# Attention's loads on GpSimd's DMA queue, and its result in a buffer of its own, in a hybrid diffusion layer

## Chip, cores and metric

One core of one Trainium2 chip runs the whole program. The metric is device microseconds (us) from start to end of one execution; lower is better.

## The reference, cut to what matters

One layer acts on 256 context tokens and 2048 latent tokens (a grid of 32 rows by 64 columns), both 1024 wide. After a modulated RMSNorm one projection of 8192 columns feeds three mixers (attention, a gated linear recurrence, a short convolution) and the gates that merge them; two more projections and a last RMSNorm follow. Everything is float32. The part that matters here is attention with its gate:

```python
(q, k, v, g_na, u, g_lru, c_b, c_c, c_h, g_conv,
 m_na, m_lru, m_conv) = jnp.split(xm @ w_in, SPLIT_IDX, axis=-1)
...
s_loc = einsum('brnqhd,brnikhd->brnhqik', q_blk, k_band)   # 8 x 16 window in an 8 x 32 band
s_ctx = einsum('brnqhd,bchd->brnhqc', q_blk, ctx_k)        # 256 cached context keys
p = softmax(concat([s_loc * scale + bias, s_ctx * scale]))
o_na = p_loc @ v_band + p_ctx @ ctx_v
...
merged = sigmoid(m_na) * ((o_na * silu(g_na)) @ w_br_na) + ...
```

There are 8 heads of 64. Context tokens attend densely to the 256 context tokens.

## The kernel before, in words

**Dense work.** The input projection is done by `dense` (L197): `load_w` (L138) loads a tile of 128 output columns in two halves (`wraw`, L143, on SyncE's queue, SP), ScalarE casts each half to its high part `whi` (L55) and GpSimd subtracts to get the low part `wlo` (L56). `w_in_chunk` (L147) then makes 24 matmuls of 128x512 (L153; three per slice of 128 inputs, the third of which needs `wlo`) and a function of the tile moves the result out of PSUM. In the stages below that is `ev_tanh` (L164): ScalarE writes `evm` (L167) and issues its store to `d_sig` on its own DMA queue (L168).

**Side work.** Attention is a generator of units that `dense` steps through `Side.tick` (L187) between chunks. In stage A (about 650 to 1015 us of the trace: 20 tiles of 3 chunks, one unit after each chunk) it does the context tokens (`prompt_steps`, L657: 8 heads, 2 units each) and the first group of 512 latent tokens. In stage B (about 1588 to 2047 us: tiles of 2 chunks, 101/27 units after each chunk) it does the other three groups of latent tokens. Stage B begins with a call of `first_loads` (L862), two tiles with no side work, and then 14 tiles with it.

**A job** is one group of one head (L737; 8 jobs in A, 24 in B) and has four units of 128 queries. `attend1` (L575) makes the scores: two matmuls against the cached keys (`sc`, L583), two against the band (`sl`, L587), then maximum, exponential and scaling on VectorE and ScalarE (L588 to L598). `attend2` (L601) transposes the probabilities (L611) and copies them (L614), `attend3` (L618) multiplies by the values (L624). A unit's later steps lag its first by two to four units (`unit`, L628, and `advance`, L635). After a job's last unit `fin` (L757) multiplies the sums by the gate: two VectorE instructions (L761) write over `sg`, and SP stores `sg` to `d_z` (L762).

**The loads.** `load_head` (L711) loads a head's keys `kd` (L715) and cached keys `ck` (L717), `load_values` (L720) its values `vb` (L722), `load_group` (L725) a job's queries `qs` (L728), its bias `bt` where that is new (L731) and its gate `sg` (L734). They are called after unit 0 of the job before (L784 to L787; the values after unit 3, L788). `first_loads` (L739) loads what the first job needs, with `cv` (L742). In `prompt_steps`, `load` (L661) loads queries, keys and gate of a head (L665 to L667), and L672 the context values. All are issued by SP, in one queue with `wraw` and the stores. Queries come through `twice` (L654), which reads the same 64 rows of `d_q` twice, into partitions 0 to 63 and 64 to 127: its outermost dimension is a 2 that steps nowhere. `qs`, `kd`, `ck`, `vb`, `bt` have two buffers each, `sg` has five. So queries of job j+1 take the buffer of job j-1, which is free once the last `sl` matmul of job j-1 has read it.

What sets the order is each engine's own queue: an instruction that waits for a buffer or a semaphore holds up all behind it on that engine. The order in a queue follows the program's, with small shifts made when it is built.

Of the kernel before, what the change touches and what calls it, by code (L numbers as in the profile page):

```python
# [7 lines left out]
F32 = mybir.dt.float32  # L8
# [3 lines left out]
ALU = mybir.AluOpType  # L12
# [3 lines left out]
P = 128  # L16
# [11 lines left out]
HD = 64  # L28
# [16 lines left out]
def build(nc, tc, H):  # L45
    es = ExitStack()
    V, S, G, TE, SY = nc.vector, nc.scalar, nc.gpsimd, nc.tensor, nc.sync
# [3 lines left out]
    def r2f(ap):  # L51
        return ap.bitcast(F32)
# [20 lines left out]
    def scratch(name, shape):  # L73
        return tc.dram_tile(shape, F32, name=name)
# [3 lines left out]
    d_q, d_k = scratch("d_q", [512, 2, T]), scratch("d_k", [HEADS, 2, HD, T])  # L78
    d_ck = scratch("d_ck", [HEADS, 2, HD, 256])
    d_v = scratch("d_v", [NCTX, 512])  # L80


    d_vb = scratch("d_vb", [HEADS, P, 8, 4, HD])
    d_gna = scratch("d_gna", [512, T])
# [3 lines left out]
    d_z = scratch("d_z", [1536, T])  # L88
# [30 lines left out]
    def bank(name):  # L119
        return psA.tile([P, 512], F32, tag="bank", name=name, bufs=8)  # L120
# [115 lines left out]
    with tc.tile_pool(name="p0", bufs=2) as p0:  # L236
# [23 lines left out]
        for i in range(4):  # L260
            mr_ = p0.tile([P, 512], F32, tag="tm", name=f"mrow{i}", bufs=3)
            (V.tensor_copy if i % 2 else S.copy)(mr_[:2, :], pm[i][:2, :])
            for j in range(4):
                o = 2 * (4 * i + j)
# [363 lines left out]
    def unit(nm, qs, keys, bias, pv, oap, nloc, fin=None):  # L628

        p = attend1(nm, qs, keys, bias, nloc)  # L630
        pend.append((nm, p, pv, oap, fin))
        if len(pend) > DEPTH:
            advance()
# [17 lines left out]
    def rows(h):  # L651
        return slice(h * HD, h * HD + HD)

    def twice(h, t0, n):  # L654
        return d_q[rows(h), :, t0 : t0 + n].unsqueeze(0).broadcast_to([2, HD, 2, n])

    def prompt_steps(pp, first_loads):  # L657

        ts = {}

        def load(h):  # L661
            qp = pp.tile([P, 2, 256], F32R, tag="qp", name=f"qp{h}")
            kp = pp.tile([P, 256], F32R, tag="ck", name=f"kp{h}")
            sp = pp.tile([HD, 256], F32, tag="sp", name=f"sp{h}", bufs=3)
            SY.dma_start(r2f(qp), twice(h, 0, 256))  # L665
            SY.dma_start(r2f(kp), d_k[h, :, :, 0:256].rearrange("a p n -> (a p) n"))
            SY.dma_start(sp, d_gna[rows(h), 0:256])  # L667
            ts[h] = qp, kp, sp

        load(0)  # L670
        vpr = pp.tile([P, 2, 512], F32, tag="vpr", name="vpr", bufs=1)
        SY.dma_start(vpr, d_v[0:256, :].rearrange("(a p) c -> p a c", p=P))  # L672
        for _ in range(8):
            yield
        for h in range(HEADS):
            if h == 1:
                first_loads()
            if h + 1 < HEADS:
                load(h + 1)
            qp, kp, sp = ts.pop(h)  # L680
            o = bank(f"op{h}")

            def fin(sp=sp, o=o, h=h):
                for a in range(2):
                    V.scalar_tensor_tensor(sp[:, a * P : (a + 1) * P], o[a * HD : a * HD + HD, a * P : (a + 1) * P],
                                           0.5, sp[:, a * P : (a + 1) * P], ALU.mult, ALU.mult)
                SY.dma_start(d_z[rows(h), 0:256], sp)

            for a in range(2):
                def oap(q0, q1, a=a, o=o):  # L690
                    return o[a * HD : a * HD + HD, a * P + q0 : a * P + q1]
                unit(f"p{h}_{a}", [qp[:, i, a * P : (a + 1) * P] for i in (0, 1)], [kp], None,
                     [[(c * P, vpr[:, c, rows(h)], P, 0, P) for c in range(2)]], oap, 0,
                     fin if a == 1 else None)
                yield
# [6 lines left out]
    def latent_steps(at, gs):  # L702

        cv = at.tile([P, 2, 512], F32, tag="cv", name=f"cv{gs[0]}", bufs=1)
        row0 = GR[gs[0]][1]
        nrows = GR[gs[-1]][1] + GR[gs[-1]][2] - row0
        nrow_max = max(GR[g][2] for g in gs)
        nq = (nrows + 3) // 4
        heads, groups, bias = {}, {}, {}

        def load_head(h):  # L711

            kd = at.tile([P, nrows * 64], F32R, tag="kd", name=f"kd{row0}_{h}")
            t0 = 256 + row0 * 64
            SY.dma_start(r2f(kd), d_k[h, :, :, t0 : t0 + nrows * 64].rearrange("a p n -> (a p) n"))  # L715
            ck = at.tile([P, 256], F32R, tag="ck", name=f"ck{row0}_{h}")
            SY.dma_start(r2f(ck), d_ck[h].rearrange("a p n -> (a p) n"))  # L717
            heads[h] = [kd, ck, None]

        def load_values(h):  # L720
            vb = at.tile([P, nq, 4, HD], F32, tag="vb", name=f"vb{row0}_{h}")
            SY.dma_start(vb, d_vb[h][:, row0 // 4 : row0 // 4 + nq])  # L722
            heads[h][2] = vb

        def load_group(g, h):  # L725
            _, _, nrow, bi = GR[g]
            qs = at.tile([P, 2, 512], F32R, tag="qs", name=f"qs{g}_{h}")
            SY.dma_start(r2f(qs), twice(h, 256 + 512 * g, 512))  # L728
            if (bi, h) not in bias:
                bt = at.tile([P, 3, nrow_max * 32], F32, tag="bt", name=f"bt{bi}_{h}")  # L730
                SY.dma_start(bt[:, :, : nrow * 32], H[f"bias{bi}"][h])  # L731
                bias[bi, h] = bt
            sg = at.tile([HD, 512], F32, tag="sg", name=f"sg{g}_{h}", bufs=5)
            SY.dma_start(sg, d_gna[rows(h), 256 + 512 * g : 768 + 512 * g])  # L734
            groups[g, h] = qs, bias[bi, h], sg

        jobs = [(g, h) for h in range(HEADS) for g in gs]  # L737

        def first_loads():  # L739
            load_head(0)  # L740
            load_group(*jobs[0])
            SY.dma_start(cv, H["cv"].rearrange("(a p) c -> p a c", p=P))  # L742
            load_values(0)

        return first_loads, latent_units(at, jobs, heads, groups, cv, row0, load_head, load_group, load_values)

    def latent_units(at, jobs, heads, groups, cv, row0, load_head, load_group, load_values):
        for ji, (g, h) in enumerate(jobs):
            (kd, ck, vb), (qs, bt, sg) = heads[h], groups.pop((g, h))
            _, kr0, nrow, _ = GR[g]  # L750
            nloc = nrow * 32
            o = bank(f"o{h}_{g}")
            ov = o.rearrange("p (r c) -> p r c", c=64)
            kv = kd[:, (kr0 - row0) * 64 : (kr0 - row0 + nrow) * 64].rearrange("p (r c) -> p r c", c=64)
            q0_ = (kr0 - row0) // 4

            def fin(o=o, sg=sg, g=g, h=h):  # L757
                for a in (0, 1):
                    ga, oa = (x.rearrange("p (r b c) -> p r b c", b=4, c=16)[:, :, a::2, :]
                              for x in (sg, o[a * HD : a * HD + HD]))  # L760
                    V.scalar_tensor_tensor(ga, oa, 0.5, ga, ALU.mult, ALU.mult)  # L761
                SY.dma_start(d_z[rows(h), 256 + g * 512 : 256 + (g + 1) * 512], sg)  # L762

            nxt = jobs[ji + 1] if ji + 1 < len(jobs) else None
            for b in range(4):
                def oap(q0, q1, b=b, ov=ov):
                    h0 = b % 2 * HD
                    return ov[h0 : h0 + HD, q0 // 16 : q1 // 16, 16 * b : 16 * b + 16]
                pv = []
                for c, q0, q1 in FULL.get(g, MID):  # L770
                    keys = min(4, nrow - 4 * c) * 32
                    pv.append((c * P, vb[:, q0_ + c, b, :], keys, q0, q1))
                for c in range(2):
                    pv.append((nloc + c * P, cv[:, c, rows(h)], P, 0, P))

                fu = [x for x in pv if x[4] - x[3] == P]
                hv = [x for x in pv if x[4] - x[3] < P]
                pv = [fu[:3] + hv[:1], fu[3:] + hv[1:]] if len(hv) == 2 else [fu, hv]
                ct = (0, 1, 1, 2)[b]
                unit(f"{h}_{g}_{b}", [qs[:, i, b * P : (b + 1) * P] for i in (0, 1)],  # L780
                     [kv[:, :, BS[b] : BS[b] + 32], ck], bt[:, ct, :nloc], pv, oap, nloc,
                     fin if b == 3 else None)

                if nxt and b == 0:  # L784
                    if nxt[1] != h:
                        load_head(nxt[1])
                    load_group(*nxt)  # L787
                if nxt and b == 3:  # L788
                    if nxt[1] != h:
                        load_values(nxt[1])  # L790
                yield
# [118 lines left out]
    with tc.tile_pool(name="zp", bufs=2, reuse_waits="tile") as zp:  # L910
        for c in (0, 1, 2, 3, 4):
            t0, n = CH[c]
# [4 lines left out]
            for br in (2, 1, 0):  # L917
# [6 lines left out]
                for m in range(8):  # L924
                    t = zp.tile([P, 512], F32, tag="acc" if br == 2 else "tg", name=f"tg{c}_{br}_{m}",
                                bufs=9 if br == 2 else 6)
# [20 lines left out]
    with tc.tile_pool(name="op", bufs=2, reuse_waits="tile") as op:  # L947
# [17 lines left out]
        for t1, n1 in [(0, P), (P, P)] + [(256 * c, 256) for c in range(1, T // 256)]:  # L965
            if t1:
                mh, ml = nxt if t1 == P else load_m(t1, n1)
            for j in range(n1 // P):
                t0 = t1 + j * P
# [105 lines left out]
```

## Time and profile before

| what | value |
|---|---|
| median of 3 runs | 2635.49 us (2634.15 to 2640.91) |
| the profiled execution's own time | 2634.21 us |
| its span in the trace | 2632.4 us |
| PE (TensorE matmul) busy | 2542.0 us, 97% of the span |
| DVE (VectorE), ACT (ScalarE), POOL (GpSimd) busy | 1092.2, 977.5, 720.6 us |
| moved by DMA | 360.55 MB, mean 137 GB/s |

Times are us unless marked ns. PEld is TensorE's weight load. A name such as `qs<-d_q` is output<-input; L728 is a line of the kernel; SPq and ACTq are the instruction queues of SyncE and ScalarE when they issue DMAs. The time of a DMA issue is how long it held its queue, not how long the data took. A busy figure counts no DMA issues. PEclk is the granted TensorE clock as a share of 2.4 GHz; the levels are 2.4 and 1.2 GHz, so 0.93 is a mean over stretches at 1 and at 0.5.

### The profile page before, as it was taken

Reading aid. Unit: us, or ns where it says so; the run is one execution under the profiler, and the core shown is the slowest. Engines: PE = TensorE matmul, PEld = TensorE weight load, DVE = VectorE, ACT = ScalarE, POOL = GpSimd, SP = SyncE. Lnnn points to the kernel's source line nnn. Section 1 sums busy time; section 2 is a strip of 40 time slices with the busy share of each in tenths; the row PEclk is TensorE's granted clock in tenths of the full one; section 3 lists DMA queues with packets and bytes.
Section 4 is the critical chain, followed back from the end, with each engine's and each line's share of the span. In section 5 each row is a group of like instructions: output and inputs, shape, how many; then the busy total and the mean of one; then the engine's idle time right before and its main releaser. Section 6 shows DMA issues by size and latency. Waiting matters only on the chain.

```text
span 2632.4 us, 35267 instructions
## 1 busy us (share of the span) xinstructions
PE 2542.0 (97%) x13192; PEld 2077.3 (79%) x13192; DVE 1092.2 (41%) x2329; ACT 977.5 (37%) x1849; POOL 720.6 (27%) x594
## 2 busy tenths in 40 slices
PE   8999999999699999999999998899889999999998
PEld 4887788888688888888888886677677888888887
DVE  5101344555023332324877862445445134333433
ACT  4312353444133334435665653344444311111221
POOL 2311223332111111521544441000000413334642
PEclk9999999999899999999999998999999999999999
DMA  7335642332533433335643335444442466545442
GB/s 272 111 90 154 180 113 79 74 69 68 156 118 123 138 123 142 125 107 139 185 157 99 114 120 167 131 140 145 142 132 91 142 216 217 176 156 172 165 144 88
DMA packets 228796, 360.55 MB, mean 137 GB/s; under 512 B 55945, under 2 KB 100617, under 8 KB 227601
## 3 DMA queue, kind: packets, MB, share of 16 engines
q1 hardware_dynamic: 175264, 291.17, 36.4%
q10 hardware_dynamic: 53360, 67.13, 7.6%
q8 instruction: 104, 1.70, 0.3%
q14 instruction: 68, 0.55, 0.1%
HBM read 248.10 MB, written 110.11 MB: 136 GB/s over the span
## 4 chain that ended last, share of the span: by engine, by line
PE 77%; DMA 9%; SPq 1%; DVE 1%; ACT 1%; issue 0%; POOL 0%; ACTq 0%; DVEq 0%; POOLq 0%
PE ps L153 45%; PE pb L931 12%; PE po L980 8%; DMA qs<-d_q 5%; PE t L611 3%; PE o L624 3%; PE pg L454 2%; PE pv L321 2%; PE sl L587 1%; PE sc L583 1%; DMA bt<-bias 1%; DMA kd<-d_k 1%; DMA cv<-cv 1%; DMA o_st<-h 0%; SPq L734 0%
## 5 line engine op out<-in xcount | busy, mean ns | idle before, releaser
L153 PE MATMUL ps<-xh,whi 128*128 128x512 f32 (+1 forms) x2400 | 898.1, 374 | 0.0
L153 PE MATMUL ps<-xl,whi 128*128 128x512 f32 (+1 forms) x2400 | 887.5, 370 | 2.1 <-DVE xl L56 1.6
L153 PE MATMUL ps<-xh,wlo 128*128 128x512 f32 (+1 forms) x2400 | 886.9, 370 | 0.0
L56 POOL TENSOR_TENSOR wlo<-wraw,whi 128x512 fp32r<-128x512 f32 x240 | 333.8, 1408 | 1085.6 <-ACT whi L55 998.6
L153 PEld LDWEIGHTS ps<-xh,whi 128*128 128x128 f32 x2400 | 454.5, 189 | 93.1 <-ACT qo L367 5.2
L153 PEld LDWEIGHTS ps<-xl,whi 128*128 128x128 f32 x2400 | 454.8, 189 | 78.3 <-POOL xl L56 2.5
L153 PEld LDWEIGHTS ps<-xh,wlo 128*128 128x128 f32 x2400 | 454.4, 189 | 77.3
L55 ACT CAST whi<-wraw 128x512 fp32r<-128x512 f32 x240 | 144.8, 616 | 320.0 <-PE ps L153 182.7
L931 PE MATMUL pb<-zh,wbh 128*128 128x512 f32 (+1 forms) x480 | 179.4, 374 | 4.3 <-ACT zh L55 4.3
L931 PE MATMUL pb<-zl,wbh 128*128 128x512 f32 (+1 forms) x480 | 179.7, 374 | 0.0
L931 PE MATMUL pb<-zh,wbl 128*128 128x512 f32 (+1 forms) x480 | 179.6, 374 | 0.0
L167 ACT ACTIVATE evm<-ps 128x512 f32<-128x512 f32 (+1 forms) x120 | 66.3, 553 | 301.1 <-PE ps L153 264.9
L588 DVE TENSOR_SCALAR_CACHE_REDUCE p<-sc 128x256 f32<-128x256 f32 x127 | 53.9, 424 | 274.4 <-PE sc L583 273.5
L938 POOL TENSOR_TENSOR tg<-tg,tg 128x512 f32<-128x512 f32 (+1 forms) x80 | 97.6, 1228 | 189.4 <-DVE tg L934 183.9
L934 DVE SCALAR_TENSOR_TENSOR tg<-tg,pb 128x512 f32<-128x512 f32 (+1 forms) x120 | 75.0, 631 | 158.6 <-PE pb L931 146.2
L611 PE MATMUL t<-ident,p 128*128 128x128 f32 (+1 forms) x698 | 129.2, 285 | 3.6 <-DVE ast L595 1.6
L611 PEld LDWEIGHTS t<-ident,p 128*128 128x128 f32 (+1 forms) x698 | 91.4, 142 | 50.9 <-issue 19.7
L614 ACT COPY pT<-t 128x512 f32<-128x512 f32 (+3 forms) x256 | 96.2, 407 | 85.1 <-PE t L611 83.1
L596 ACT ACTIVATE p<-p,ast 128x736 f32<-128x736 f32 (+2 forms) x127 | 109.5, 862 | 41.8 <-DVE ast L595 38.8
L444 DVE SCALAR_TENSOR_TENSOR uf<-ut,pk,uf 128x512 f32<-128x512 f32 (+1 forms) x120 | 104.2, 868 | 31.4 <-ACT uf L441 29.4
L55 ACT CAST zh<-zr 128x512 fp32r<-128x512 f32 (+1 forms) x60 | 30.5, 575 | 213.3 <-PE pb L931 134.7
L931 PEld LDWEIGHTS pb<-zh,wbh 128*128 128x128 f32 x480 | 90.7, 189 | 22.1 <-ACT zh L55 4.8
(222 smaller groups left out, 3494.9 us busy)
## 6 DMA issues: line engine op xcount, KB each, us to landing
wraw<-w_in SPq DMA_DIRECT2D x240, 256.0 KB
d_sig<-evm ACTq DMA_DIRECT2D x96, 256.0 KB
tg<-d_sig SPq DMA_DIRECT2D x96, 256.0 KB
xt<-x SPq DMA_DIRECT2D x36, 512.0 KB
qs<-d_q SPq DMA_DIRECT2D x32, 512.0 KB
zr<-d_z SPq DMA_DIRECT2D x12, 1024.0 KB
d_mrg<-tg ACTq DMA_DIRECT2D x32, 256.0 KB
mr<-d_mrg SPq DMA_DIRECT2D x8, 1024.0 KB
```

What stands on the lines that cost most here:

```text
L55: S.copy(hi, src)
L56: lo_eng.tensor_tensor(lo, src, r2f(hi), ALU.subtract)
L153: TE.matmul(ps[:, :n], (lo if a else hi)[:, k, :], (xl if b else xh)[ci][:, k, :], start=(i == 0), stop=(i == len(ps_) - 1))
L444: V.scalar_tensor_tensor(uf[:, :n], ut[:, tap : tap + n], cw(tap), uf[:, :n], ALU.mult, ALU.add)
L596: S.activation(p[:, :nk], p[:, :nk], AF.Exp, bias=st[:, 2:3], accum_out=st[:, 3:4])
L611: TE.transpose(tb[:, off : off + w], p[q0:q1, c0 : c0 + P], ident[q0:q1, q0:q1])
L614: S.copy(pT[:, base : base + off], tb[:, :off])
L624: TE.matmul(o, lhsT, rhs, start=(i == 0), stop=(i == len(todo) - 1))
L931: TE.matmul(ps[:, :n], (wbl if a_ else wbh)[br * 4 + k][:, m * P : (m + 1) * P], (zl if b_ else zh)[:, k, :n], start=(i == 0), stop=(i == ...
L934: V.scalar_tensor_tensor(t[:, :n], t[:, :n], 1.0, ps[:, :n], ALU.add, ALU.mult)
L938: G.tensor_tensor(acc[m][:, :n], acc[m][:, :n], t[:, :n], ALU.add)
L980: TE.matmul(ps, (ml if a_ else mh)[:, k, j * P : (j + 1) * P], (wol if b_ else woh)[k][:, hs], start=(i == 0), stop=(i == len(ps_) - 1))
```

## The change

Every load of attention is issued by GpSimd's queue in place of SP's: three per head and one more in `prompt_steps`, and in the latent part `kd`, `ck`, `vb`, `qs`, `bt`, `sg` and `cv`. `fin` writes to a new tile `zt` (two buffers) and SP stores that; `sg` has three buffers in place of five. Stores and the loads of weights stay on SP. No arithmetic changes.

```diff
@@ prompt_steps, load
-            SY.dma_start(r2f(qp), twice(h, 0, 256))
-            SY.dma_start(r2f(kp), d_k[h, :, :, 0:256].rearrange("a p n -> (a p) n"))
-            SY.dma_start(sp, d_gna[rows(h), 0:256])
+            G.dma_start(r2f(qp), twice(h, 0, 256))
+            G.dma_start(r2f(kp), d_k[h, :, :, 0:256].rearrange("a p n -> (a p) n"))
+            G.dma_start(sp, d_gna[rows(h), 0:256])
...
-        SY.dma_start(vpr, d_v[0:256, :].rearrange("(a p) c -> p a c", p=P))
+        G.dma_start(vpr, d_v[0:256, :].rearrange("(a p) c -> p a c", p=P))
@@ latent_steps
-            SY.dma_start(r2f(kd), d_k[h, :, :, t0 : t0 + nrows * 64].rearrange("a p n -> (a p) n"))
+            G.dma_start(r2f(kd), d_k[h, :, :, t0 : t0 + nrows * 64].rearrange("a p n -> (a p) n"))
...
-            SY.dma_start(r2f(ck), d_ck[h].rearrange("a p n -> (a p) n"))
+            G.dma_start(r2f(ck), d_ck[h].rearrange("a p n -> (a p) n"))
...
-            SY.dma_start(vb, d_vb[h][:, row0 // 4 : row0 // 4 + nq])
+            G.dma_start(vb, d_vb[h][:, row0 // 4 : row0 // 4 + nq])
...
-            SY.dma_start(r2f(qs), twice(h, 256 + 512 * g, 512))
+            G.dma_start(r2f(qs), twice(h, 256 + 512 * g, 512))
...
-                SY.dma_start(bt[:, :, : nrow * 32], H[f"bias{bi}"][h])
+                G.dma_start(bt[:, :, : nrow * 32], H[f"bias{bi}"][h])
...
-            sg = at.tile([HD, 512], F32, tag="sg", name=f"sg{g}_{h}", bufs=5)
-            SY.dma_start(sg, d_gna[rows(h), 256 + 512 * g : 768 + 512 * g])
+            sg = at.tile([HD, 512], F32, tag="sg", name=f"sg{g}_{h}", bufs=3)
+            G.dma_start(sg, d_gna[rows(h), 256 + 512 * g : 768 + 512 * g])
...
-            SY.dma_start(cv, H["cv"].rearrange("(a p) c -> p a c", p=P))
+            G.dma_start(cv, H["cv"].rearrange("(a p) c -> p a c", p=P))
@@ latent_units, fin
+                zt = at.tile([HD, 512], F32, tag="zt", name=f"zt{g}_{h}")
                 for a in (0, 1):
-                    ga, oa = (x.rearrange("p (r b c) -> p r b c", b=4, c=16)[:, :, a::2, :]
-                              for x in (sg, o[a * HD : a * HD + HD]))
-                    V.scalar_tensor_tensor(ga, oa, 0.5, ga, ALU.mult, ALU.mult)
-                SY.dma_start(d_z[rows(h), 256 + g * 512 : 256 + (g + 1) * 512], sg)
+                    za, ga, oa = (x.rearrange("p (r b c) -> p r b c", b=4, c=16)[:, :, a::2, :]
+                                  for x in (zt, sg, o[a * HD : a * HD + HD]))
+                    V.scalar_tensor_tensor(za, oa, 0.5, ga, ALU.mult, ALU.mult)
+                SY.dma_start(d_z[rows(h), 256 + g * 512 : 256 + (g + 1) * 512], zt)
```

## Rows read from the trace of the kernel before

**Rows 1.** Page, part 1: span, busy us (share of the span), instructions.
```profile
span 2632.4 us, 35267 instructions
PE 2542.0 (97%) x13192; PEld 2077.3 (79%) x13192; DVE 1092.2 (41%) x2329; ACT 977.5 (37%) x1849; POOL 720.6 (27%) x594
```

**Rows 2.** Windows of stages A and B; columns in the first line.
```profile
core 0: us, PE busy (x) PEld busy (x) DVE busy (x) ACT busy (x) POOL busy (x), PEclk, DMA share, GB/s
650.00:1015.00 365.00, 343.93 (x2112) 293.48 (x2111) 92.12 (x341) 115.11 (x274) 49.27 (x39) 0.97 0.41 127
1588.00:2047.00 459.00, 416.32 (x2715) 325.77 (x2714) 196.54 (x719) 190.79 (x446) 38.87 (x31) 0.93 0.43 135
```

**Rows 3.** Waits of PE in stage B: us in total, times, longest us.
```profile
PE sc L583 <- DMA qs<-d_q: 35.0, 9, 7.4
```

**Rows 4.** Windows of three moments: in A, and two in B.
```profile
680.00:720.00 40.00, 19.89 (x103) 17.14 (x102) 2.66 (x10) 6.01 (x14) 5.03 (x4) 0.78 0.60 171
1757.00:1760.00 3.00, 0.00 (x0) 0.00 (x0) 0.00 (x0) 0.00 (x0) 0.00 (x0) 0.53 0.13 51
1641.00:1643.00 2.00, 1.54 (x20) 1.21 (x21) 0.12 (x2) 1.91 (x4) 1.21 (x1) 1.00 0.14 54
```

**Rows 5.** DMA queues from 1641 to 1643: packets, MB, share of 16 engines.
```profile
q1 hardware_dynamic: 50, 0.10, 13.0%
```

**Rows 6.** Chain of work that ended last, in order: start us, us, what.
```profile
1591.18 20.24 DMA qs<-d_q
...
1742.43 18.00 DMA qs<-d_q
...
1845.78 17.35 DMA qs<-d_q
...
1912.31 8.30 DMA d_z<-sg
```

**Rows 7.** Waits of SP's queue in stage B: us in total, times, longest us.
```profile
SPq L734 <- DMA d_z<-sg: 154.8, 19, 14.6
SPq L143 <- POOL wlo L56: 51.4, 15, 10.9
SPq L762 <- DVE sg L761: 22.6, 2, 11.6
```

**Rows 8.** Timeline of SP's queue in stage B: start us, us held.
```profile
1611.43 8.01 SPq L734 DMA_DIRECT2D sg<-d_gna  x1
...
1637.19 7.38 SPq L143 DMA_DIRECT2D wraw<-w_in  x3
```

**Rows 9.** The last band matmuls of a job, and all issues of latent queries.
```profile
L587 PE MATMUL sl<-kd,qs x2: 383/383/383, 1838.2 to 1838.5; 128*128 128x480 f32 x2
L728 SPq DMA_DIRECT2D qs<-d_q x32: 532/540/1895, 671.8 to 2003.8; - x32
```

**Rows 10.** Timeline of ACT in stage A: start us, us, what, [idle before <-releaser].
```profile
696.08 0.60 ACT L167 ACTIVATE evm<-ps 128x512 f32<-128x512 f32 x1 [1.10 <-DMA sp<-d_gna]
713.62 0.33 ACTq L168 DMA_DIRECT2D d_sig<-evm  x1
714.05 0.60 ACT L167 ACTIVATE evm<-ps 128x512 f32<-128x512 f32 x1 [17.37 <-DMA bt<-bias]
```

**Rows 11.** Timeline of one low-part pair on POOL and the matmul that needs it.
```profile
1802.94 2.51 POOL L56 TENSOR_TENSOR wlo<-wraw,whi 128x512 fp32r<-128x512 f32 x2 [27.60 <-ACT whi L55]
...
1809.79 0.50 PE L153 MATMUL ps<-xh,whi 128*128 128x512 f32 x1
```

**Rows 12.** Stage B by line: busy us, mean ns | idle before.
```profile
L598 DVE TENSOR_SCALAR p<-p,ast 128x736 f32<-128x736 f32 (+1 forms) x95 | 55.4, 583 | 1.3
L761 DVE SCALAR_TENSOR_TENSOR sg<-o,sg 64x256 f32<-64x256 f32 x48 | 20.2, 420 | 25.5 <-PE o L624 24.9
```

## The prediction

> **What bounds the kernel now.** I read the page's first part, then windows by stage, then the waits of the engine that has no slack. TensorE is busy for 97% of the span [rows 1], so a change that does no arithmetic can only win where TensorE stands still or runs at the lower clock. In the two attention stages that is 365 - 343.9 = 21.1 us in A and 459 - 416.3 = 42.7 us in B [rows 2]. The granted clock averages 0.93 in B; with levels 1 and 0.5 that is 0.14 of 459, some 64 us at 1.2 GHz. Outside these stages the change touches nothing. So no more than 21 + 43 us and what the low clock costs is to be had.
>
> In B the standing is one wait: the first score matmul of a job waits for its queries, nine times, 35.0 us in all [rows 3]. The chain shows why a query load is slow: 17 to 20 us from issue to landing for 512 KB [rows 6]. At 1757 to 1760, where TensorE does nothing, the DMA engines are 13% busy and move 51 GB/s: 0.13 x 16 is two engines [rows 4]. At 1641 to 1643 SP's queue moves 50 packets for 0.10 MB at 13.0% [rows 5], so 256 packets of 2 KB take 256/50 x 2 = 10.2 us at best. The other 7 us are what lies ahead in the same two engines' queues, and the latency. The two engines also hold up those who come behind: at 1637 to 1644.6, with the DMA engines 14% busy at 1641 to 1643, SP was stuck for 7.38 us issuing weight loads [rows 4, 8].
>
> The second loss is that queries are asked for late. In the example the last band matmul that reads the buffer starts at 1838.5 [rows 9], and the load that takes the buffer is issued at 1845.78 [rows 6], 7 us later. SP was not idle: its queue waits 154.8 us at the gate load L734, 22.6 us at the store L762 for VectorE and 51.4 us at weights [rows 7], and one that waits holds all behind it.
>
> In A the standing is one gap: 680 to 720 has 19.9 us of TensorE in 40 [rows 4]. ScalarE wrote an `evm` at 696.08, could issue the store of it at 713.62 only, and the next `evm` counts 17.37 us of waiting for a bias load [rows 10]. No data joins the two; what joins them must be how landings are counted or queued. With ScalarE stuck PSUM isn't emptied and TensorE stops.
>
> **The change part by part.** *Issues moved.* From the code: A moves 8 x 3 + 1 in `prompt_steps` and 8 x 6 + 1 in the latent part, 74; B moves 24 qs, 24 sg, 16 bt, 8 each of kd, ck, vb and one cv, 89. GpSimd issues no DMA in the kernel before, so the price of one is unknown. Bounds: 0 (only if GpSimd's engine doesn't wait for it) and 8.01 us, the longest issue on SP [rows 8]; nearest is SP's median query issue, 0.54 us [rows 9]. I take 1 us, double that, since GpSimd also computes. That is 89 us on GpSimd in B beside 38.9 us of work in 459, and 74 beside 49.3 in 365 [rows 2]: no engine becomes full.
>
> *What they are moved past.* On GpSimd they stand between the `wlo` subtractions. A pair of these ended at 1805.45, and the matmuls that need it began at 1809.79 [rows 11]: 4.3 us of cover. Four issues of a job take 4 us, just covered; with a new head's keys it is six. B has 27 chunks for 101 units, 7.5 units per tile, and loads after every fourth, so of 13 tile boundaries 3 follow a load at once: 3 x 2 = 6 us lost. In A a unit comes only every 365/48 = 7.6 us: 2 us. Sum **+8**. The new wait, GpSimd at the query load until the buffer is free, holds the same `wlo`; it ends as the next job begins, and is in this count.
>
> *The late asking.* The first of the nine waits, 7.4 us [rows 3], belongs to the start of B, where the first load lands 20 us after its issue [rows 6]; keys and queries still go first in one queue, so I leave it. Of the other 27.6 us I take two thirds, **-18**: the queue that issues queries no longer holds weights and stores, the 7 us lag goes to about 2, and backlog on the two engines shrinks as weights and stores lie in another queue. What would be late next is the 10.2 us transfer itself: issue 1, latency about 2 (an estimate: part of the 7 us beyond the transfer), in all some 13 us, against a job of (416 - 20 - 23)/24 = 15.5 us (20 lost to the clock, below; 23 for four chunks before the side work). It fits barely, which is why a third stays. Bounds: 0 and -27.6.
>
> *The stall of A.* If landings of GpSimd's loads are kept apart from those of ScalarE's stores, the 20 us gap goes; a burst of some 17 loads at the stage's start remains on GpSimd. **-16**; bounds 0 and -20.
>
> *The clock.* The stretch 1757 to 1760 stands at 0.53 [rows 4]: the fall follows the standing. Of B's 64 us at 1.2 GHz I put 24 as idle inside (over half of the 42.7), so 40 us of work took double: 20 us lost. Half the gaps' causes go: **-10**; bounds 0 and -20.
>
> *The new buffer.* `fin` has the same two VectorE instructions of 420 ns [rows 12] with another output: 0. The gate load no longer waits for a store to land. With three `sg` buffers the load after unit 0 of job j needs `fin` of job j-2, which the program puts after unit 2 of job j-1, two units earlier: hidden. `zt` waits for the store two jobs back, 8.3 us [rows 6] against 2 x 15.5; without that cover VectorE would wait there. 0.
>
> Sum: -16 - 18 - 10 + 8 = **-36**. The profiled execution's own time is 2634.2 (span 2632.4 [rows 1]), 1.3 under the median of 2635.5. 2634.2 - 36 = **2598 us**.
>
> The Trainium skill (DMA: Bandwidth & Descriptors, Rules for kernel authors) says that an outermost dimension of c copies keeps a whole DMA on at most c engines, whichever queue issues it. The two engines of the trace agree, and by that rule the 10.2 us stay.
>
> **The rivals.** *Queries spread out.* If GpSimd's queue puts a query load on more engines, or on other ones each time, it lands in a few us (51 GB/s from two engines is 408 from sixteen: 1.3 us, and the latency). Then all 27.6 us go, 20 of the clock, 20 in A and 5 of B's start: 2634 - 73 + 8 = 2569. For it: nothing in the rows ties the two engines to the data's shape rather than to SP's queue. Against: the leading 2 is unchanged.
>
> *VectorE holds GpSimd up.* If a long VectorE instruction such as L598, 583 ns a time [rows 12], keeps GpSimd from issuing, each of 24 query loads in B loses up to 0.58 us, 14 in all: 2612. For and against: no row has GpSimd issue a DMA.
> The Trainium skill (SBUF — State Buffer, section "SBUF: two separate sides", the box on the "DVE blocks DMA" trap) has such a lock, for VectorE's two-port operations while GpSimd writes descriptors; no run here shows it yet.
>
> *Only the queue changes its name.* GpSimd already waits 27.60 us for ScalarE ahead of a pair [rows 11]; a query load behind that wait is as late as now, and A's gap may be the burst itself. Then only a few us move: 2631. Against: SP's waits at stores and weights do fall away.
>
> *Slower: GpSimd's issues starve the weights.* Mechanism: `wlo` behind a group of loads, TensorE waits for its third matmul. It decides from about 2 us an issue, where a group of four takes 8 and passes the cover by far. At 3 us: 12 + 2.5 - 4.3 = 10 us at each of 3 boundaries of B, 8 at 4 more that follow one unit (2.2 us) later, 62; in A 5 boundaries by 3 us, 15; and queries come 3 us later, so the gains shrink to 34. 2634 + 77 - 34 = 2677. For it: GpSimd needs 2.51 us for a pair [rows 11], so any issue ahead of one is felt late; against: 89 issues are few in 459 us.
>
> **How the numbers follow.** Forecast 0.42, queries spread 0.22, VectorE's lock 0.08, same 0.12, starved 0.16. The range 2550 to 2648 holds the forecast with its bounds (-74 + 8 gives 2568; 0 + 8 gives 2642), the spread case with some room, and the unchanged one; most of the starved case lies outside. This kernel's measurement can tell 0.3%, 8 us, from no change. Faster by more: 0.40 of the forecast, 0.22, 0.07 of the lock and 0.03 of the unchanged case, 0.72. Within: 0.01 + 0.01 + 0.08, 0.10. Slower: the starved 0.16 and 0.02 of the forecast and the unchanged case, 0.18.
>
> **What would show it.** Right: the wait of L583 for queries falls from 35 to some 15 us, query issues lie within 2 us of the last band matmul, the gap at 680 to 720 is gone, SP's longest waits are short, and while queries load alone the DMA share is still 0.13. Spread: that share is far above, landings in a few us. Same: a wait of GpSimd at L728 or L56 in place of SP's at L734. Starved: PE L153 waits for `wlo`, GpSimd's queue is held for over 2 us an issue. Wrong altogether: TensorE's idle in A and B unchanged while the time differs.

## The result, and the profile after

The changed kernel takes 2611.05 us (median of 4 runs, 2610.51 to 2611.97), the one before 2635.51 beside it. The ratio is 0.9905 [0.989, 0.992], 24.5 us less. The forecast was 2598 us in a range of 2550 to 2648: the sign was right and the gain, forecast at 36 us, is two thirds of that. The profiled executions differ by 2634.21 - 2611.47 = 22.7 us. From `fin` on, lines of the new kernel are one higher: its store is L763, its two products L762.

The page's first part of the kernel after:

```profile
span 2609.7 us, 35312 instructions
PE 2542.3 (97%) x13192; PEld 2077.4 (80%) x13192; DVE 1104.2 (42%) x2329; ACT 978.3 (37%) x1849; POOL 876.7 (34%) x757
```

TensorE is busy as long as before [rows 1]; GpSimd has 163 instructions and 156.1 us more, 0.96 us for each load that it now issues (busy time here takes its DMA issues in). To place the gain I cut each stage from the last `pg` matmul ahead of it to its last `o` matmul. Windows of A and B, before:

```profile
645.50:1015.00 369.50, 348.43 (x2131) 297.17 (x2131) 94.91 (x346) 119.59 (x282) 51.76 (x41) 0.97 0.41 126
1576.90:2046.90 470.00, 427.32 (x2763) 334.81 (x2763) 202.91 (x728) 198.31 (x456) 42.26 (x34) 0.93 0.43 134
```

and after, with the 40 us of A that held the gap:

```profile
680.00:720.00 40.00, 39.15 (x221) 33.66 (x220) 7.94 (x32) 11.52 (x30) 18.70 (x18) 1.00 0.66 193
646.50:1000.50 354.00, 348.24 (x2131) 296.18 (x2130) 100.39 (x346) 119.81 (x282) 118.15 (x115) 1.00 0.45 132
1562.70:2025.30 462.60, 427.81 (x2763) 335.77 (x2762) 211.26 (x728) 198.94 (x456) 133.07 (x123) 0.94 0.47 137
```

A is 15.5 us shorter and B 7.4, which is all of it. In both, TensorE's busy time is what it was (348.4 and 348.2; 427.3 and 427.8): the gain is standing time alone, 21.1 to 5.8 us in A and 42.7 to 34.8 in B, and the low clock of B gave nothing back. The gap of A is gone: 39.15 of its 40 us are busy, against 19.89 [rows 4].

B is the riddle. Waits of TensorE there, after (us in total, times, longest):

```profile
PE sc L583 <- DMA qs<-d_q: 20.5, 6, 9.0
PE t L611 <- DVE ast L597: 4.1, 1, 4.1
```

35.0 us [rows 3] became 20.5, and the longest wait grew. What TensorE stands for besides queries grew as well, from 42.7 - 35.0 = 7.7 us to 34.8 - 20.5 = 14.3, so B's standing fell by 7.9 us and not by 14.5. Are queries still asked for late? GpSimd's timeline around one load (start us, us held, what, idle before and its releaser):

```profile
1836.02 2.28 POOL L728 DMA_DIRECT2D qs<-d_q  x1 [13.47 <-PE sl L587]
1838.30 0.54 POOL L734 DMA_DIRECT2D sg<-d_gna  x1
1838.81 0.79 POOL L731 DMA_DIRECT2D bt<-bias  x1
1842.94 2.51 POOL L56 TENSOR_TENSOR wlo<-wraw,whi 128x512 fp32r<-128x512 f32 x2 [3.34 <-ACT whi L55]
```

No: GpSimd stands ready for 13.47 us, and the last band matmul itself (L587) releases the load. It is so throughout: 22 loads of B take the buffer of an earlier job of B, and they are issued 0.3 to 1.1 us after the end of the last band matmul that reads it; before the change that took 0 to 13.6 us, 3.5 on average. All 32 query loads, their time on GpSimd and from issue to landing:

```profile
L728 POOL DMA_DIRECT2D qs<-d_q x32: 2102/2111/2342, 669.2 to 1979.6; - x32
...
DMA to landing us min/median/max: 14.8/17.1/24.6
```

The chain of waits shows the same from the other side (start us, us):

```profile
1648.53 19.60 DMA qs<-d_q
...
1856.97 18.42 DMA qs<-d_q
...
1912.75 18.55 DMA qs<-d_q
...
1965.14 16.56 DMA qs<-d_q
```

A load asked for in time and landing 17 us later does not fit a job of 15.5 us. The load is still on two engines, and it doesn't have them to itself. From 1848 to 1851 the load issued at 1836.02 is under way and GpSimd issues nothing else; the queues of GpSimd (q0), SP (q1) and ScalarE (q10) moved (packets, MB, share of 16 engines)

```profile
q0 software_dynamic: 22, 0.09, 7.4%
q1 hardware_dynamic: 22, 0.04, 3.3%
q10 hardware_dynamic: 15, 0.03, 2.3%
```

Together that is 13.0% of 16, again two engines [rows 4, 5], and the load has little over one of them (7.4% of 16 is 1.2). Its packets are larger than on SP's queue (0.09 MB in 22, against 0.10 in 50 [rows 5]); the speed of an engine is not, some 25 GB/s in both.

### The profile page after: what moved, and what is told of

Read it like the earlier page. It is cut to its first block, busy times and chain, and to the rows that moved or that the text cites. A ratio compares the mean times of both kernels' runs of the same rounds, so it can differ in the third digit from the quotient of the medians.

```text
span 2609.7 us, 35312 instructions
## 1 busy us (share of the span) xinstructions
PE 2542.3 (97%) x13192; PEld 2077.4 (80%) x13192; DVE 1104.2 (42%) x2329; ACT 978.3 (37%) x1849; POOL 876.7 (34%) x757
## 2 busy tenths in 40 slices
DMA packets 248812, 360.84 MB, mean 138 GB/s; under 512 B 88761, under 2 KB 124729, under 8 KB 247617
## 3 DMA queue, kind: packets, MB, share of 16 engines
q1 hardware_dynamic: 147360, 227.20, 28.7%
## 4 chain that ended last, share of the span: by engine, by line
PE 75%; DMA 6%; issue 4%; POOL 2%; DVE 1%; ACT 0%; SPq 0%; ACTq 0%; POOLq 0%; DVEq 0%
PE ps L153 45%; PE pb L932 12%; PE po L981 8%; DMA qs<-d_q 3%; PE t L611 3%; PE o L624 2%; PE pg L454 2%; PE pv L321 1%; PE sl L587 1%; PE sc L583 1%; DMA bt<-bias 1%; DMA d_z<-sp 1%; POOL wlo L56 0%; DMA kp<-d_k 0%; DMA d_q<-evl 0%
## 5 line engine op out<-in xcount | busy, mean ns | idle before, releaser
L153 PE MATMUL ps<-xh,whi 128*128 128x512 f32 (+1 forms) x2400 | 899.6, 375 | 0.0
L153 PE MATMUL ps<-xl,whi 128*128 128x512 f32 (+1 forms) x2400 | 888.8, 370 | 2.4 <-DVE xl L56 1.6
L153 PE MATMUL ps<-xh,wlo 128*128 128x512 f32 (+1 forms) x2400 | 888.2, 370 | 0.0
L153 PEld LDWEIGHTS ps<-xh,whi 128*128 128x128 f32 x2400 | 455.2, 190 | 93.7 <-issue 6.2
L153 PEld LDWEIGHTS ps<-xh,wlo 128*128 128x128 f32 x2400 | 455.1, 190 | 78.1
L153 PEld LDWEIGHTS ps<-xl,whi 128*128 128x128 f32 x2400 | 455.2, 190 | 77.8 <-POOL xl L56 2.0
L475 POOL TENSOR_TENSOR sq<-sq,ea 128x512 f32<-128x512 f32 (+1 forms) x40 | 61.9, 1548 | 154.2 <-ACT sq L468 92.6
## 6 DMA issues: line engine op xcount, KB each, us to landing
qs<-d_q POOLq DMA_DIRECT2D x32, 512.0 KB, 17.1
```

What stands on the lines that cost most here:

```text
L153: TE.matmul(ps[:, :n], (lo if a else hi)[:, k, :], (xl if b else xh)[ci][:, k, :], start=(i == 0), stop=(i == len(ps_) - 1))
```

## The experiments

All stages are cut as above; a stage's length and TensorE's standing time in it are of one profile each, and differences under some 5 us in them are not settled. Ratios are to the kernel before, run beside each.

| kernel | us | ratio [95%] | A: length, idle | B: length, idle |
|---|---|---|---|---|
| before | 2635.5 | 1 | 369.3, 21.1 | 469.9, 42.7 |
| after | 2611.1 | 0.9905 [0.989, 0.992] | 353.8, 5.8 | 462.6, 34.8 |
| a_only | 2612.7 | 0.9905 [0.989, 0.9919] | 356.2, 8.0 | 462.6, 32.7 |
| b_only | 2629.2 | 0.9963 [0.995, 0.9976] | 370.6, 21.2 | 463.0, 36.0 |
| zt_only | 2625.9 | 0.9951 [0.9937, 0.9965] | 367.9, 20.0 | 466.2, 35.6 |
| g_no_zt | 2622.3 | 0.9938 [0.9917, 0.996] | 359.7, 9.1 | 464.8, 39.8 |
| lat_a | 2632.7 | 0.9974 [0.9963, 0.9985] | 362.7, 11.8 | 470.8, 42.1 |
| q_on_g | 2651.0 | 1.004 [1.0024, 1.0057] | 354.1, 6.4 | 493.3, 66.0 |
| rest_on_g | 2654.7 | 1.005 [1.0033, 1.0067] | 382.0, 29.2 | 475.6, 51.8 |
| qs3_sp | 2656.8 | 1.0059 [1.004, 1.0078] | 379.2, 28.7 | 481.1, 56.8 |
| split_sp | 2554.2 | 0.9684 [0.967, 0.9699] | 345.3, 0.0 | 412.9, 5.6 |
| split_g | 2559.5 | 0.9709 [0.9693, 0.9725] | 346.4, 0.6 | 417.3, 8.4 |
| split_sp_zt | 2555.2 | 0.9673 [0.9657, 0.969] | 345.3, 0.0 | 411.4, 5.6 |

**Which stage: a_only and b_only.** The new buffer in both; in a_only the loads of A go to GpSimd and those of B stay on SP, in b_only the other way round.

```diff
+        LQ = G if gs[0] == 0 else SY        # a_only; reversed in b_only, where prompt_steps stays on SY
...
-            SY.dma_start(r2f(qs), twice(h, 256 + 512 * g, 512))
+            LQ.dma_start(r2f(qs), twice(h, 256 + 512 * g, 512))
```

> Stage A's loads (context tokens and first latent group) on GpSimd, stage B's back on SP; the new buffer stays in both. Theory (two separate gains, 14 us in A and 7 us in B, read from where the stages end in the two traces): about 2635 - 14 = 2621 us, the 20 us gap at 680 to 720 gone, B's TensorE idle as before, near 43 us. Rival (one gain, the freed queue of SP, which comes with the whole move): under a third of 24 us, 2627 or more. If the new buffer alone matters in B: 2614.

> Stage B's loads on GpSimd, stage A's and the context tokens' on SP. Theory (separate gains): 2635 - 7 = 2628 us, the gap of 20 us in A still there, queries in B issued within 2 us of their buffer coming free, landing still 16 to 19 us after issue. Rival (the stages share one gain): 2620 or less, or 2635.

a_only is as fast as the whole change. So in the presence of the new buffer, moving B's loads is worth nothing, and B's 7 us come without it: B is 462.6 us long with its loads on SP. b_only keeps A's gap (18.1 us of its 21.2) and gains 10 us.

**The new buffer alone: zt_only, and the queue alone: g_no_zt.**

```diff
+                zt = at.tile([HD, 512], F32, tag="zt", name=f"zt{g}_{h}")      # zt_only: all loads on SY
...
-                SY.dma_start(d_z[rows(h), 256 + g * 512 : 256 + (g + 1) * 512], sg)
+                SY.dma_start(d_z[rows(h), 256 + g * 512 : 256 + (g + 1) * 512], zt)
```

> The new buffer and three gate buffers alone; every load stays on SP. Theory (the 7 us of stage B come from the new buffer: a gate load on SP no longer waits for a store to land, so SP asks for queries in time; B was as long with its loads on SP as on GpSimd once the buffer was there): stage B 463 us as in the changed kernel, stage A 370 as before, 2635 - 7 = 2628 us, and SP's 155 us of waiting at the gate load gone. Rival (B's 7 us need loads off SP in stage A or B): B at 470, 2635.

> All loads of attention on GpSimd, but attention's result written over its gate and five gate buffers, as before. Theory (A's gain is the queue's, B's the buffer's): A 354 us, B at 470 or, with GpSimd held at the gate load by a store of SP's, more: 2635 - 15 = 2620 us. Rival (the queue alone gives both): 2611. Rival (GpSimd held at the gate load starves the weights' low parts): over 2635.

The buffer that I costed at nothing gains half a per cent without the move. Waits of TensorE, then of SP's queue, in B of zt_only:

```profile
PE sc L583 <- DMA qs<-d_q: 25.9, 8, 6.2
```

```profile
SPq L143 <- POOL wlo L56: 61.1, 19, 10.9
SPq L728 <- PE t L611: 42.5, 16, 14.9
```

SP's 154.8 us at the gate load [rows 7] are gone; the query load now stands at the head of SP's queue and waits for TensorE, as it does on GpSimd after the change. Its issue follows the end of the band matmul that frees its buffer by 0.8 us on average in zt_only and by 0.9 in g_no_zt, where it was 3.5. So queries were late because the gate load, ahead of them on SP, waited for the store of an in-place result to land. In the queue as built a gate load doesn't stand behind its own queries, as in `load_group`, but five jobs ahead, behind the store that frees its buffer. In the kernel before (start us, us held):

```profile
1877.00 0.46 SPq L762 DMA_DIRECT2D d_z<-sg  x1
1880.58 0.46 SPq L734 DMA_DIRECT2D sg<-d_gna  x1
...
1881.77 0.54 SPq L728 DMA_DIRECT2D qs<-d_q  x1
```

Taking that wait away and taking the queries off that queue do the same thing (B is 466.2 us long with the one, 464.8 with the other), and the second adds little where the first is done.

From the ratios, at about 2637 us: the buffer is -13 us (0.9951); A's loads on top of it -12 (0.9905); B's loads on top of the buffer +3 (0.9963; the intervals overlap), on top of both 0. Without the buffer the two moves together give -16 (0.9938). The buffer's 13 us are of its median; its profiled run shows 2634.21 - 2629.25 = 5, 1.4 of them in A and 3.7 in B (that run is slower than its kernel's median, 2625.88). zt_only has three gate buffers in place of five, too, as the change has; no run has `zt` with five. Three with the result in place did not take SP's wait away (qs3_sp, below).

**What closes A's gap: lat_a and q_on_g.** lat_a moves only A's latent loads (LQ as above, no new buffer, `prompt_steps` on SP); q_on_g moves only the two query loads, in both stages.

```diff
-            SY.dma_start(r2f(qp), twice(h, 0, 256))
+            G.dma_start(r2f(qp), twice(h, 0, 256))
...
-            SY.dma_start(r2f(qs), twice(h, 256 + 512 * g, 512))
+            G.dma_start(r2f(qs), twice(h, 256 + 512 * g, 512))
```

> Only the latent loads of stage A on GpSimd; the context tokens' and all of stage B's on SP, no new buffer. Theory (in A ScalarE's stores were held until the latent group's early loads, bias and queries not needed for another 80 us, had landed): gap of 20 us gone, A about 355, B 470, 2620 us. Rival (it is the context tokens' own loads that hold things up): A at 369, 2635.

> Only the query loads (both kinds) on GpSimd, all else as before. Theory (the query loads' two engines are what backs up SP's queue and ScalarE's stores): A's gap gone as with the whole change, and SP not held at issues of 7 us; B between 455 and 463, since keys, values and bias no longer stand in one queue with the queries: 2605 to 2613 us. Rival (all loads must leave): A over 365, 2625 or more.

In lat_a the gap of 20.1 us becomes 4.9 and 5.5 (the time was 2632.7 us, where I had written 2620), in q_on_g 3.4 and 2.3: the query loads of both parts make it. The program's own listing says what joins them to ScalarE's store (row in its engine's order, and the semaphores that it waits for). Before, on SP and on ScalarE:

```
SP   328 L731 DMA bt_1_6533<-bias 128x1056 [waits DMAHW2_49]
ACT  518 L168 DMA d_sig<-evm 128x512 [waits DMAHW2_49,Activation_49]
```

after, on GpSimd:

```
POOL 175 L728 DMA qs_0_5754<-d_q 128x2x512 [waits DMASW0_49,Pool_49]
```

In this listing landings of SP's and ScalarE's DMAs are counted on the same eight counters, and a DMA waits until the one before it on its counter has landed. The bias load behind a query load lands late, and the store next on that counter waits 17 us for it [rows 10]: a row of the trace and a semaphore that agree. GpSimd's loads have counters of their own.

But q_on_g, which I had put at 2605 to 2613 us, is slower than before, and B tells why. Its chain, and the queues and issues from 1877 to 1901 (the load issued at 1876.86):

```profile
1654.10 24.16 DMA qs<-d_q
...
1876.86 24.59 DMA qs<-d_q
1919.82 15.41 DMA qs<-d_q
1935.41 23.95 DMA qs<-d_q
```

```profile
q1 hardware_dynamic: 1292, 3.35, 46.4%
q0 software_dynamic: 1872, 0.73, 13.4%
...
kd<-d_k SPq DMA_DIRECT2D x1, 896.0 KB, 6.9
vb<-d_vb SPq DMA_DIRECT2D x1, 896.0 KB
bt<-bias SPq DMA_DIRECT2D x1, 576.0 KB, 10.4
```

Loads that begin with a new head's keys, values and bias take 24 us, the one between two heads 15. In the kernel after, the same bulk stands behind the query load in one queue, and its loads at a new head take 18 (1856.97, 1912.75). On two queues the bulk is served beside it, on its two engines as on the others. The Trainium skill (DMA: Bandwidth & Descriptors, Queues, rings and completion order) has each engine take turns between its queues by packets; that fits the kernel after, where GpSimd's queue and SP's sent 22 packets each from 1848 to 1851.

**The converse: rest_on_g.** The change, with only the queries back on SP (the two lines of q_on_g in the other direction).

> The changed kernel with only the query loads back on SP; keys, values, bias and gates stay on GpSimd, the new buffer stays. Theory (a load that has two engines shares each of them with whatever the other queue sends, so queries land late when keys, values and bias go through another queue, however early they are asked for): landing of queries over 20 us, stage B 475 us or more, as with the queries alone on GpSimd (493), 2630 to 2650. Rival (GpSimd's issue of queries is what is slow: 2.1 us, and their many small packets; SP issues them in 0.54): stage B under 460, 2605 or less.

Slower too, by as much: query waits of 45.5 us in B, though every query load there is issued as its buffer comes free (those in the chain take 16 to 33 us to land), and A's gap is back (20.8 us), with ScalarE's 18.2 us now put down to the `qp` load. SP's queue shows one more price (start us, us held):

```profile
1605.97 16.04 SPq L728 DMA_DIRECT2D qs<-d_q  x2
1622.11 18.21 SPq L143 DMA_DIRECT2D wraw<-w_in  x1
```

With nothing else between them two query loads stand one behind the other, and they and the weights behind them hold SP for 34 us. Both halves of the move are worse than none or all.

**A third query buffer instead: qs3_sp.** Everything on SP, result in place, three gate buffers as in the change.

```diff
-            qs = at.tile([P, 2, 512], F32R, tag="qs", name=f"qs{g}_{h}")
+            qs = at.tile([P, 2, 512], F32R, tag="qs", name=f"qs{g}_{h}", bufs=3)
...
-            sg = at.tile([HD, 512], F32, tag="sg", name=f"sg{g}_{h}", bufs=5)
+            sg = at.tile([HD, 512], F32, tag="sg", name=f"sg{g}_{h}", bufs=3)
```

> The kernel before with three query buffers (and three gate buffers, to make room), all loads on SP: queries can be asked for a whole job earlier and may take 30 us. Theory (TensorE waits in B because a load of 17 us must fit in one job of 15.5): stage B falls to 425 to 445, the wait of L583 for queries under 12 us; A stays near 369, as its gap hangs on landings: 2595 to 2615. Rival (the two engines also hold up keys, values and bias behind the queries, so an earlier ask moves the wait to these): B over 455, 2622 or more.

Waits of TensorE in B:

```profile
PE o L624 <- ACT pT L614: 19.7, 3, 15.1
PE t L611 <- DVE ast L595: 17.7, 4, 13.6
PE t L611 <- DVE p L598: 10.4, 8, 6.4
PE sc L583 <- DMA qs<-d_q: 6.8, 2, 5.8
```

VectorE's wait for the bias there (1.6 us before), and SP's first wait:

```profile
DVE p L590 <- DMA bt<-bias: 33.7, 6, 16.5
SPq L734 <- DMA d_z<-sg: 174.6, 21, 15.7
```

Queries are hardly waited for any more, and the kernel is slower: the wait went to the steps behind the scores, which wait for the bias, as the rival had it; whether the two engines or SP's queue kept the bias late is not shown. SP's wait at the gate load grew from 154.8 to 174.6 us. Two things changed at once (one query buffer more, two gate buffers fewer), so which of them moved it stays open.

**The transfer itself: split_sp, split_g and split_sp_zt.** Each query load as two loads of 64 rows, without the leading 2; on SP in the kernel before, on GpSimd in the kernel after, and on SP with the new buffer.

```diff
-            SY.dma_start(r2f(qs), twice(h, 256 + 512 * g, 512))
+            for a in (0, 1):
+                SY.dma_start(r2f(qs[a * HD : a * HD + HD]), d_q[rows(h), :, 256 + 512 * g : 768 + 512 * g])
```

> The kernel before, with each query load issued as two loads of 64 rows, without the leading dimension of 2; all loads stay on SP. Theory (two engines per query load are what B waits for, and what backs up SP's queue and with it ScalarE's stores in A): landing of queries falls from some 17 us to 5 or less, DMA share while queries load is far above 0.13, TensorE's idle in B falls from 43 to under 15 and the gap in A shrinks: 2635 - 27 - 10 (clock) - 10 = 2588, at least under 2605. Rival (the late asking in SP's queue is what matters, the transfer is only second): 2620 to 2630. Rival (one more issue per job costs SP as much as it gives): 2635 or more.

> The changed kernel, with each query load issued as two loads of 64 rows on GpSimd's queue. Theory (what is left in B, 35 us of TensorE's idle and the low clock behind it, is the two-engine transfer): queries land within 6 us, idle in B under 15 us, 2611 - 20 - 10 = 2581, and the issue of two half loads takes GpSimd about 1.1 us in place of 2.1. Rival (what is left is the crowd of keys, values and bias at each new head, which fills the engines): 2605 to 2611.

> Query loads in two halves of 64 rows and the new buffer, all loads on SP. With the halves alone the time was 2554. Theory (with short loads no queue is late, so neither the buffer nor the queue matters): 2552 to 2557, the same as the halves alone. Rival (SP's wait at the gate load for a store still costs): 2547 or less.

split_sp is faster than both kernels, 3.2% below the one before and 2.2% below the one after, with no queue moved and no buffer added, and by more than either forecast for the halves had it (2588 on SP, 2581 on GpSimd). Its windows, A and B, and the landing of its query loads from the page (count, size, median us):

```profile
1553.40:1966.40 413.00, 407.41 (x2763) 320.52 (x2763) 202.78 (x728) 197.95 (x456) 42.50 (x34) 1.00 0.50 153
646.00:991.50 345.50, 345.50 (x2132) 295.14 (x2132) 94.26 (x346) 119.49 (x282) 51.97 (x41) 1.00 0.46 135
```

```profile
qs<-d_q SPq DMA_DIRECT2D x64, 256.0 KB, 5.0
```

TensorE never stands in A, 5.6 us in B, and its first waits there (all of them) are not for queries:

```profile
PE t L611 <- DVE p_first L598: 2.4, 1, 2.4
PE t L611 <- DVE p L598: 1.9, 8, 0.3
PE t L611 <- DVE ast L595: 0.9, 4, 0.3
```

Standing falls by 37 us in B, and busy time by 427.3 - 407.4 = 20 us, because the granted clock is now 1.00. Once the loads land in 5 us, the buffer (0.9673 against 0.9684) is worth nothing and GpSimd's queue costs a little (0.9709 in split_g, against 0.9673 in split_sp_zt with the same buffer on SP). That the dimension of 2 keeps the load on two engines, which the prediction cited beside [rows 4, 5], is what split_sp undoes, and the landing falls from 17 us and more [rows 6] to 5.

## Why the prediction was right, and where it was not

*A, -16, of which the past-the-weights term took 2 back: right.* -12 us by ratio (a_only over zt_only), -15.5 in the profiles. "How landings are counted" was the right guess, and the listing and four kernels bear it out. What is left of A's standing, 5.8 us, isn't the burst of loads at the stage's start, as I had it. Nearly all of it is a wait for the context tokens' keys, and GpSimd's queue shows why (TensorE's wait in A; two issues of GpSimd):

```profile
PE scp L583 <- DMA kp<-d_k: 5.3, 4, 3.0
741.62 0.54 POOL L667 DMA_DIRECT2D sp<-d_gna  x1 [8.52 <-DMA d_z<-sp]
742.14 0.58 POOL L666 DMA_DIRECT2D kp<-d_k  x1
```

The context tokens' result is still written over its gate `sp`, so the gate load waits for a store to land and holds the keys behind it: the same pattern that `zt` took out of B.

*Late asking, -18 by a landing of 13 us: failed.* The first half held: each query load in B is issued within 1.1 us of its buffer coming free. The second half, "backlog on the two engines shrinks as weights and stores lie in another queue", is the step that failed. The landing stayed at 17.1 us (14.8 at the least), where I had written 13. Another queue is no other engine: the weights and stores still pass through those two (1848 to 1851, above), and B moves data at a share of 0.47 of all engines. An estimate from these rows: 24 query loads of 10.2 us on two engines are 24 x 10.2 x 2 / 16 / 462.6 = 0.07 of that; if the two carry the other 0.40 as the rest do, the transfer takes 10.2 / 0.60 = 17 us. I had counted the queue ahead of a load and not the traffic beside it. Wait for queries: 20.5 us, where I wrote some 15.

*The clock, -10: failed, 0.* Busy time in B did not change (427.3, 427.8). The 20 us that I counted as lost to 1.2 GHz are there, and split_sp gets them back; that takes the gaps gone, not fewer.

*New buffer, 0: failed.* I costed the gate load's freedom as hidden work of the buffer, and looked only for what it might cost; the 154.8 us of [rows 7] that hold the queries up were its own. It is worth 13 us by ratio, and with it B's move is worth nothing. So of the sum the queue move in B, -18 + 6 - 10 = -22, measured 0 to +3, the buffer -13 in place of 0, and A -12 in place of -14: -25 for -36. The two errors partly cancelled, since both terms priced one wait; that the sum came as near as it did is in part luck. The range's lower end has a slip: the bounds of the terms add up to -27.6 - 20 - 20 = -67.6, not -74. Nothing hung on it, as the range was put wider.

*Issues, 1 us each, and +8 for the weights behind them: the price right, the loss not paid.* 0.96 us on average. No wait of L153 for `wlo` is among TensorE's waits in B; the 4.3 us of cover [rows 11] were enough. The starved rival needed over 2 us an issue; only the query load has that (2.11).

*The other rivals.* Queries spread out: refuted (two engines, above), though the time that it gave, 2569, is near what split_sp shows the mechanism to be worth. VectorE's lock: not in the direction that I priced. An instruction of 583 ns [rows 12] in the way would show in the spread of the query issues, 2102 to 2342 ns, which is 240; plain loads of attention's latent part have medians of 0.54 to 0.58 us. The box on the trap in the Trainium skill (SBUF — State Buffer, "SBUF: two separate sides") speaks of such a lock on GpSimd; no query issue here shows it. What the trace shows is the opposite, VectorE held by GpSimd:

```profile
1751.83 2.11 POOL L728 DMA_DIRECT2D qs<-d_q  x1
1752.13 2.09 DVE L598 TENSOR_SCALAR p<-p,ast 128x640 f32<-128x640 f32 x1
1754.60 0.53 DVE L598 TENSOR_SCALAR p<-p,ast 128x640 f32<-128x640 f32 x1
```

The instruction that begins during the query issue ends with it, and the same one later takes 0.53 us. In B eight of the 96 executions of L598 took 1.0 to 2.2 us, four begun in a query issue and four in a `wlo` subtraction; before, none took over 0.61. Together they take 65.0 us in place of 56.0. How much of TensorE's other waits, 7.7 to 14.3 us, comes from that no run separates.

Only the queue changes its name: refuted for A, and for B nearer than my forecast, since a_only without B's move is as fast.

*The signs.* "SP's longest waits are short" was a bad one: SP now waits for `wlo` and for VectorE at stores, up to 27.6 us, and it costs nothing because nothing urgent stands behind.

## What to carry to other kernels

Before a load is moved to another queue, read how many engines it uses: share of the DMA engines times 16 while it runs alone. Here a load on two of them landed in some 17 us from either queue, and in up to 24 where its neighbours came from another one; reshape it (here two half loads, -3.2%) before queues and buffers are touched. And when a queue waits long at one instruction, price removing that wait before pricing the removal of everything behind it: the two are often the same microseconds.

## What was not expected of the hardware

A DMA on GpSimd's queue has its own price by shape: 0.54 us for a gate load, 2.11 for a query load, against 0.54 for that on SP [rows 9]. The page after counts 88761 packets under 512 B where the kernel before has 55945, 32816 more:

```profile
DMA packets 248812, 360.84 MB, mean 138 GB/s; under 512 B 88761, under 2 KB 124729, under 8 KB 247617
```

split_g, on the same queue without the leading 2, has 57144 of them, and 612 ns an issue. So most of the small packets and the long issue belong to the doubled load on this queue: the queue without it (split_g) has neither, nor has the doubled load on SP.
